# Summing the shift columns of w_ada two chunks at a time in a fused hybrid decoder layer

## The chip, the cores and the metric

The kernel runs on one core of one Trainium2 chip. The metric is the device time of one execution in microseconds (us). Before the change it is 1836.45 us, the median of three executions (1835.40, 1836.45 and 1836.54).

## The reference

One decoder layer over x of 1024 rows and 2048 columns, all in float32:

- `mod = silu(c) @ w_ada + b_ada`, cut into shift, scale and gate of 2048 numbers each; w_ada has 2048 rows and 6144 columns
- `h = rms_norm(x, norm_gain) * (1 + scale) + shift`
- `proj = h @ w_in` with 8192 columns: q, k, v, z of a stick-breaking attention (8 heads of 128) and of a chunkwise retention (8 heads of 128)
- both groups of heads, each multiplied by silu of its z
- `out = x + gate * (concat @ w_out)`

The change concerns the first line alone, and of it the 2048 numbers of shift.

## The kernel before

A float32 product is made of three matmuls on TensorE (PE): both operands are cut into a high and a low part, and high by high, high by low and low by high are added in one PSUM bank (`mm3`, L205 to L208). Cutting takes one copy on ScalarE (ACT, L193) and one subtraction on VectorE (DVE, L195).

Before the large projection the kernel computes seven heads' worth of columns (the retention's q, NZ = 7) directly, while it still prepares everything else. This is done in two passes of 16 steps each: the first over the upper 512 rows of x (L930), the second over the lower 512 rows (L1012). In step p of a pass, PE makes 7 times 3 matmuls with one 128-row piece of w_in (`start_mm`, the loop variable i counts the seven heads). Between them the second pass does the following, at fixed values of i:

- at the start of a step: load the two tiles of w_in of step p + 2 (`load_w`, tile name wr, called wr(p + 2) below), and in even steps a chunk of w_ada (`load_ada`). A chunk is 256 columns of w_ada in 8 tiles (name ada), each brought by its own DMA of 256 KB
- i = 0: four transposes of x into PSUM (`x_turn`, L601, tile xtp), copied out by ACT (L607); the copy of step p is that of x piece p + 2, called xT(p + 2)
- i = 2: the two parts of the scaled x piece (`make_h`, L652 on ACT, L654 on DVE)
- i = 3, even steps: `ada_mod`, which turns a chunk's sums by two transposes (L634) and reduces them on DVE (L637, L645) to 256 numbers of shift; in steps 2, 6, 10, 14 also `factors`, which queues further work that needs four pieces of shift
- i = 4, odd steps: `ada_sums` of the next chunk (L617 to L624): 16 matmuls of silu(c) with the chunk into one bank, four groups of 32 partitions, then a DVE copy of 128 by 256
- i = 4 and 6: cut wr(p + 2) (`cut_w`, L193 and L195)
- at most values of i: `pieces()`, one ACT and one DVE instruction of the queued work. Its parts end in stores of factors to DRAM (`store`, L382 and L383): for each k a pair B22h, B22l, then T1h, T1l, then T2h, T2l, called B22(k), T1(k), T2(k)

`x_turn`, `ada_sums` and `ada_mod` all write into the one PSUM bank with tag "C" (one buffer): each waits until the bank's former content has been read. In the second pass every engine's instructions, and the DMA issues on SyncE's queue (SP), run in the order in which the code states them (L982: `manual_schedule()`).

Of the 16 chunks the first eight give scale, the last eight (numbers 8 to 15) shift. Chunk 8 is summed in step 14 of the first pass and turned in step 0 of the second; chunk 9 is summed in step 1 and turned in step 2; chunk 8 + n is summed in step 2n - 1 and turned in step 2n. Chunks 8 and 9 are loaded in the first pass, chunk 10 between the passes, chunks 11 to 15 at the start of steps 2, 4, 6, 8 and 10. SBUF tiles come from a list of 92 slots, the one free longest being taken first (`Slots`).

Of the kernel before, what the change touches and what calls it, by code (L numbers as in the profile page):

```python
# [12 lines left out]
F32 = mybir.dt.float32  # L13
# [3 lines left out]
ALU = mybir.AluOpType  # L17

P = 128
S = 1024  # L20
D = 2048
KC = D // P
# [5 lines left out]
HALF = 512  # L28
# [23 lines left out]
CHUNKS = (0, 4, 1, 5, 2, 6, 3, 7)  # L52

KCS1 = (0, 1, 2, 3, 8, 9, 10, 11, 4, 5, 6, 7, 12, 13, 14, 15)
CHUNKS1 = (0, 1, 4, 5, 2, 3, 6, 7)
# [7 lines left out]
class Slots:  # L63
# [21 lines left out]
    def get(self, name, cls=None, dtype=F32, borrow=False):  # L85
        assert self.free, (name, cls, self.used)
        if cls in ("raw", "ring") and self.share and not (borrow or self.loose):
            assert self.used.get(cls, 0) < self.share[cls], (name, cls, self.used)
        i = self.free.popleft()
        self.used[cls] = self.used.get(cls, 0) + 1  # L90
        t = self.pool.tile([P, HALF], dtype, tag=f"s{i}", name=name)
        self.of[id(t)] = (t, i, cls)
        return t

    def put(self, *tiles):
        for t in tiles:
            _, i, cls = self.of.pop(id(t))
            self.used[cls] -= 1
            self.free.append(i)
# [3 lines left out]
def layer_kernel(ctx, tc, x, c, w_ada, b_ada, norm_gain, w_in, sb_q_gain, sb_k_gain, ret_norm_gain, w_out,  # L103
                 rot, ret_mask, ret_kdec, chunk_decay, out):
    nc = tc.nc
# [7 lines left out]
    sm = ctx.enter_context(tc.tile_pool(name="sm", bufs=2))  # L113
    om_pool = ctx.enter_context(tc.tile_pool(name="om", bufs=2))
    ps = ctx.enter_context(tc.tile_pool(name="ps", bufs=1, space=PS))
    dr = ctx.enter_context(tc.tile_pool(name="dr", bufs=1, space=bass.MemoryType.DRAM))
    get, put = slots.get, slots.put
# [25 lines left out]
    ident = cons.tile([P, P], F32, name="ident")  # L143
# [24 lines left out]
    gain_c = cols[:, 0:16]  # L168
    shift_b = cols[:, 16:32]
# [365 lines left out]
    shift = cons.tile([P, KC], F32, name="shift")  # L535
    qb = cons.tile([P, 2, NH], F32, name="qb")
    nc.vector.memset(qb, 0.0)
    ada, xT = {}, {}
# [6 lines left out]
    def load_ada(cc, gs=range(8)):  # L545

        col = (D + CHUNKS1[cc] * 2 * P) if cc < 8 else CHUNKS[cc - 8] * 2 * P
        for g in gs:
            ada[cc, g] = ar = get(f"ada_{cc}_{g}")
            nc.sync.dma_start(ar.rearrange("p (j n) -> p j n", n=2 * P),  # L550
                              ada_rows[:, 2 * g:2 * g + 2, col:col + 2 * P])
# [58 lines left out]
    silu_z = silu_t.rearrange("p (j n) -> p j n", n=32)  # L610
# [3 lines left out]
    def ada_sums(cc):  # L614


        ap_ = ps.tile([P, 256], F32, tag="C", name=f"accp_{cc}")  # L617
        for j in range(16):
            g = j % 4
            nc.tensor.matmul(ap_[32 * g:32 * g + 32, :], silu_z[:, j, :],  # L620
                             ada[cc, j // 2][:, (j % 2) * 256:(j % 2) * 256 + 256], start=j < 4, stop=j >= 12)
        put(*[ada.pop((cc, g)) for g in range(8)])
        acc = get(f"acc_{cc}")
        nc.vector.tensor_copy(acc[:, 0:256], ap_)  # L624
        return acc

    mods = cons.tile([P, KC], F32, name="mods")
    scale_b1 = cons.tile([P, KC], F32, name="scale_b1")

    def ada_mod(cc, acc):  # L630

        turned = ps.tile([P, 2 * P], F32, tag="C", name=f"mod_{cc}")
        for s in range(2):
            nc.tensor.transpose(turned[:, s * P:(s + 1) * P], acc[:, s * P:(s + 1) * P], ident)  # L634
        put(acc)
        mod = sm.tile([P, 2], F32, tag="mod", name=f"mod_s_{cc}")
        nc.vector.tensor_reduce(mod, turned.rearrange("p (s g r) -> p s g r", s=2, r=32)[:, :, :, 0],  # L637
                                mybir.AxisListType.X, ALU.add)
        k0 = 2 * (CHUNKS1[cc] if cc < 8 else CHUNKS[cc - 8])
        k2 = slice(k0, k0 + 2)  # L640
        if cc < 8:
            nc.vector.tensor_tensor(mods[:, k2], mod, scale_b1[:, k2], op=ALU.add)
            nc.vector.tensor_tensor(mods[:, k2], mods[:, k2], gain_c[:, k2], op=ALU.mult)
        else:
            nc.vector.tensor_tensor(shift[:, k2], mod, shift_b[:, k2], op=ALU.add)  # L645

    def make_h(p, hf):

# [122 lines left out]
    def start_mm(p, hf, ws, heads):  # L771
        kc = (KCS if hf else KCS1)[p]
        for h in heads:
            if p == 0:
                tag, bufs = starter_tags[h]
                first[h] = ps.tile([P, HALF], F32, tag=tag, bufs=bufs, name=f"first_{h}_{hf}")
            hi, lo = ws[h // 4]
            sl = slice(h % 4 * P, (h % 4 + 1) * P)
            mm3(first[h], hi[:, sl], lo[:, sl], h_hi[kc, hf], h_lo[kc, hf], p == 0, p == KC - 1)
# [110 lines left out]
    sums = {}  # L890
# [39 lines left out]
    for p in range(KC):  # L930
        c = p // 2
        if p == WRITTEN:
            written.close()
        loads(p)
        w = ws.pop(p)
        for h in range(NZ):
            start_mm(p, 0, w, (h,))
            if p < WRITTEN:
                s = p + 1
                if s < 4 and h == 2:  # L940
                    first_acc = first_sums(s)
                if s < 4 and h == 3:
                    first_mod(s, first_acc)
                    ws[s] = [cut_w(s, 0, raw[s], 0)]
                    make_h(s, 0)
                if p in (3, 5) and h == 1:
                    sums[c + 1] = ada_sums(c + 1)
                if p in (3, 5) and h == 2:
                    ada_mod(c + 1, sums.pop(c + 1))
                if (p, h) in TURNS:  # L950
                    x_turn(TURNS[p, h], 0, "C", 1)
                if (p, h) in SQUARES:
                    squares(SQUARES[p, h][0], SQUARES[p, h][1:])
                if s >= 4 and h == 4:
                    make_h(s, 0)
                    ws[s] = [cut_w(s, 0, raw[s], 0)]
                if h == (4 if s < 4 else 5):
                    ws[s].append(cut_w(s, 0, raw[s], 1))
                    put(*raw.pop(s))
                continue  # L960
            if (p, h) in TURNS:
                x_turn(TURNS[p, h], 0, "C", 1)
            if p >= KC - 2 and h == 1:
                x_turn(p - KC + 2, 1, "C", 1)
                make_h(p - KC + 2, 1)
            if p % 2 == 0 and h == 3:
                sums[c + 1] = ada_sums(c + 1)
            if p % 2 and p < KC - 1 and h == 0:
                ada_mod(c + 1, sums.pop(c + 1))
            if p == 12 and h == 3:  # L970
                norm_wide = norm_columns()
            if p == 13 and h == 5:
                norm_row = norm_rows(norm_wide)
            if h == 4 and p < KC - 1:
                make_h(p + 1, 0)
        put(h_hi.pop((KCS1[p], 0)), h_lo.pop((KCS1[p], 0)))
# [35 lines left out]
    for p in range(KC):  # L1012
        cc = 8 + p // 2
        if 2 <= p < KC - 2:
            rawz[p + 2] = load_w(p + 2, 1)
        if p and p % 2 == 0 and cc + 2 < 16:
            load_ada(cc + 2)
        if p >= 12:
            for _ in range(3):
                if early:  # L1020
                    b, hh, q = early.popleft()
                    load_raw(0, q, b, hh)
        w, cuts = ws.pop(p), []
        heads = range(NZ) if p < KC - 1 else (3, 0, 1, 2, 4, 5, 6)
        for i, h in enumerate(heads):
            start_mm(p, 1, w, (h,))
            if p == 1 and i or p > 1 and i < 2:
                scale_some(1)
            if i == 0 and p + 2 < KC:
                x_turn(p + 2, 1, "C", 1)  # L1030
            if i == 2 and p + 2 < KC:
                make_h(p + 2, 1)
            if i == 3 and p % 2 == 0:
                ada_mod(cc, sums.pop(cc))
            if i == 4 and p % 2 and cc < 15:
                sums[cc + 1] = ada_sums(cc + 1)
            if i == 3 and p % 4 == 2:
                factors((KCS[p - 2], KCS[p - 1]))
            if i in (4, 6) and p + 2 < KC:
                cuts.append(cut_w(p + 2, 1, rawz[p + 2], i // 2 - 2))  # L1040
            if i not in (2, 4):
                pieces()
            if p == KC - 1:
                if i:
                    spill(heads[i - 1], 1)
                if i in (1, 3, 5):
                    prepare_entry(i // 2)
        put(h_hi.pop((KCS[p], 1)), h_lo.pop((KCS[p], 1)))
        if p + 2 < KC:
            ws[p + 2] = cuts  # L1050
            put(*rawz.pop(p + 2))
# [658 lines left out]
    C = {2: (0, 0), 5: (1, 1), 3: (0, 1), 4: (1, 0)}  # L1710
# [281 lines left out]
    for i, (prod, ms, k) in enumerate(steps):  # L1992
# [16 lines left out]
        for m in ms:  # L2009
            for t in range(4):  # L2010
                b = 4 * m + t
                if k == 0 and prod not in (6, 5, 3):
                    tag, bufs = ("pj", 4) if prod == 7 else tags[b]
                    out_banks[b] = ps.tile([P, HALF], F32, tag=tag, bufs=bufs, name=f"y_{prod}_{b}")
                tk = slice(t * P, (t + 1) * P)
                for d in range(2 if both else 1):
                    l, r = lcut[i + d], rcut[i + d, m]
# [78 lines left out]
```

## Time and profile before

| what | value |
|---|---|
| median of three executions | 1836.45 us |
| the profiled execution | 1835.84 us |
| its span, first to last instruction | 1834.1 us |
| granted TensorE clock, mean | 0.999 |
| DVE busy | 1388.3 us (76%) |
| ACT busy | 872.4 us (48%) |
| main DMA queue, share of 16 engines | 88.0% |

The span is what lies between the first and the last instruction; 1.74 us of the execution lie around it. In a row of the timeline the first number is the start in us from the span's beginning and the second the time from the first start to the last end of the instructions merged in it. Successive matmuls overlap, so what a matmul costs is read from the distance between starts, not from its own duration. SPq rows are DMA issues: their length is the time to issue, and the data land later.

### The profile page before, as it was taken

What the parts mean: (1) busy time and instruction counts of PE and PEld (TensorE: products, weight loads), DVE (VectorE), ACT (ScalarE), POOL (GpSimd) and SP (SyncE); (2) the same over time, 40 slices, a digit from 0 to 9 for tenths busy, and PEclk for the clock granted to TensorE, in tenths of its full rate; (3) what the DMA queues carried; (4) which work ended last, traced back from release to release, by engine and by line L of the source; (5) the groups of instructions that cost most, each with busy time, mean ns of one, the idle gap of its engine ahead of it and who ended that gap; (6) DMA issues with size and microseconds to landing.
All of it is one profiled execution on the core that took longest, in us unless ns stands there. A gap on an engine that the chain in (4) does not pass through costs nothing.

```text
span 1834.1 us, 28370 instructions
## 1 busy us (share of the span) xinstructions
PE 1822.9 (99%) x9268; PEld 1501.3 (82%) x9268; DVE 1388.3 (76%) x2653; ACT 872.4 (48%) x1659; POOL 84.0 (5%) x226
## 2 busy tenths in 40 slices
PE   8999999999999999999999999999999999999999
PEld 6777788888888888878888888888888888888887
DVE  3578875666878777877778686988798777687697
ACT  3647852234554455435543554445545565452231
POOL 0000000000100010000010101000000001000000
PEclk9999999999999999999999999999999999999999
DMA  9998999998799699978997899889998864994694
GB/s 293 355 362 266 325 353 365 376 356 304 223 317 309 241 301 307 318 268 292 306 332 258 304 294 306 305 281 308 343 332 275 307 207 150 369 343 165 216 307 159
DMA packets 441112, 541.00 MB, mean 295 GB/s; under 512 B 33658, under 2 KB 246020, under 8 KB 440964
## 3 DMA queue, kind: packets, MB, share of 16 engines
q1 hardware_dynamic: 440148, 538.78, 88.0%
q8 instruction: 73, 1.20, 0.3%
q14 instruction: 75, 0.61, 0.1%
q10 hardware_dynamic: 816, 0.40, 0.1%
HBM read 448.83 MB, written 90.22 MB: 294 GB/s over the span
## 4 chain that ended last, share of the span: by engine, by line
PE 51%; ACT 0%; DMA 0%; DVE 0%; issue 0%; DVEq 0%
PE pj L206 10%; PE pj L208 9%; PE pj L207 9%; PE y L208 5%; PE y L206 5%; PE y L207 5%; PE sp L1577 1%; PE op L1596 1%; PE op L1598 1%; PE up L1559 1%; PE tp_B L1366 0%; PE oT L206 0%; PE oT L208 0%; PE oT L207 0%; PE zp L206 0%; PE zp L208 0%
## 5 line engine op out<-in xcount | busy, mean ns | idle before, releaser
L195 DVE TENSOR_TENSOR wl<-A,wh 128x512 fp32r<-128x512 f32 x392 | 270.6, 691 | 188.1 <-ACT wh L193 177.8
L193 ACT ACTIVATE wh<-A 128x512 fp32r<-128x512 f32 x392 | 247.1, 631 | 337.7 <-PE pj L207 319.8
L417 ACT ACTIVATE c<-pj 128x512 f32<-128x512 f32 x112 | 66.5, 598 | 120.8 <-PE pj L208 118.0
L316 DVE TENSOR_TENSOR A<-A,A 128x512 f32<-128x512 f32 x160 | 108.8, 686 | 1.7
L1330 ACT ACTIVATE om<-zp,y 128x128 f32<-128x128 f32 (+2 forms) x96 | 55.6, 579 | 104.1 <-PE zp L208 64.0
L421 DVE TENSOR_TENSOR c<-pj,c 128x512 f32<-128x512 f32 x104 | 69.8, 687 | 38.8 <-PE pj L208 38.6
L206 PE MATMUL first<-h_hi,wh_first 128*128 128x512 f32 x224 | 94.6, 423 | 0.8 <-ACT h_hi L652 0.8
L1346 DVE TENSOR_TENSOR_SCAN om<-om 128x128 f32<-128x128 f32 (+2 forms) x96 | 93.7, 976 | 1.1
L206 PE MATMUL pj<-T1h,wh 128*128 128x512 f32 x232 | 94.2, 406 | 0.0
L206 PE MATMUL pj<-B22h,wh 128*128 128x512 f32 x232 | 92.7, 400 | 0.0
L206 PE MATMUL pj<-B21h,wh 128*128 128x512 f32 x232 | 92.6, 399 | 0.0
L206 PE MATMUL pj<-B11h,wh 128*128 128x512 f32 x232 | 91.3, 393 | 0.0
L208 PE MATMUL pj<-T1h,wl 128*128 128x512 f32 x232 | 90.8, 391 | 0.0
L208 PE MATMUL pj<-B22h,wl 128*128 128x512 f32 x232 | 90.6, 391 | 0.0
L208 PE MATMUL pj<-B21h,wl 128*128 128x512 f32 x232 | 90.6, 391 | 0.0
L207 PE MATMUL pj<-B21l,wh 128*128 128x512 f32 x232 | 90.4, 390 | 0.0
L207 PE MATMUL pj<-T1l,wh 128*128 128x512 f32 x232 | 90.4, 390 | 0.0
L208 PE MATMUL pj<-B11h,wl 128*128 128x512 f32 x232 | 90.4, 390 | 0.0
L207 PE MATMUL pj<-B22l,wh 128*128 128x512 f32 x232 | 90.3, 389 | 0.0
L207 PE MATMUL pj<-B11l,wh 128*128 128x512 f32 x232 | 90.3, 389 | 0.0
L206 PE MATMUL pj<-T3h,wh 128*128 128x512 f32 x224 | 89.8, 401 | 0.0
L206 PE MATMUL pj<-T4h,wh 128*128 128x512 f32 x224 | 89.5, 400 | 0.0
(427 smaller groups left out, 4967.7 us busy)
## 6 DMA issues: line engine op xcount, KB each, us to landing
A<-in_w_in_dram SPq DMA_DIRECT2D x228, 256.0 KB, 5.6
ada<-in_w_ada_dram SPq DMA_DIRECT2D x112, 256.0 KB, 5.6
wB<-in_w_out_dram SPq DMA_DIRECT2D x112, 256.0 KB, 5.7
gr<-in_w_ada_dram SPq DMA_DIRECT2D x64, 256.0 KB, 5.5
T2h<-fac_T SPq DMA_DIRECT2D x56, 256.0 KB, 5.3
T2l<-fac_T SPq DMA_DIRECT2D x56, 256.0 KB, 5.8
T1h<-fac_T SPq DMA_DIRECT2D x56, 256.0 KB, 5.1
T1l<-fac_T SPq DMA_DIRECT2D x56, 256.0 KB, 5.5
```

What stands on the lines that cost most here:

```text
L193: nc.scalar.activation(hi[:, 0:n], src[:, 0:n], AF.Copy)
L195: nc.vector.tensor_tensor(lo[:, 0:n], src[:, 0:n], hi[:, 0:n].bitcast(F32), op=ALU.subtract)
L206: nc.tensor.matmul(o, a_hi, b_hi, start=first, stop=False, skip_group_check=on)
L207: nc.tensor.matmul(o, a_hi, b_lo, start=False, stop=False, skip_group_check=on)
L208: nc.tensor.matmul(o, a_lo, b_hi, start=False, stop=last, skip_group_check=on)
L316: nc.vector.tensor_tensor(r[o], r[a], r[b], op=ALU.add if n == 1 else ALU.subtract)
L417: nc.scalar.activation(order(t), o, AF.Copy)
L421: nc.vector.tensor_tensor(t, o, t, op=ALU.add)
L1330: nc.scalar.activation(om[:, :n], zp[:, :n], AF.Sigmoid, scale=y[:, 16 + i:17 + i])
L1346: nc.vector.tensor_tensor_scan(rev, rev, rev, init, op0=ALU.mult, op1=ALU.bypass)
L1559: nc.tensor.matmul(up[:, j * P:(j + 1) * P], kd[:, j * P:(j + 1) * P], vb(4 * g + j), start=True, stop=True)
L1577: nc.tensor.matmul(sp[:, j, :], r["k", g][:, tk], r["q", g][:, tk], start=True, stop=True)
```

## The change

`ada_sums2` sums two chunks of shift into one bank of 512 columns and copies them out in one instruction; `ada_shift2` turns both by four transposes, reduces them in one instruction and adds the bias in two. The two are called once in four steps of the second pass: the sums in steps 1, 5, 9 and 13 at i = 4, for chunks 8 and 9, 10 and 11, 12 and 13, 14 and 15; the turning in steps 2, 6, 10 and 14 at i = 3. Chunk 8 is no longer summed in the first pass. The loads move: chunk 11 from step 2 to step 3, chunk 12 from step 4 to step 5 (behind its sums), chunk 13 from step 6 to step 7, chunk 14 from step 8 to step 9 (behind its sums), chunk 15 from step 10 to step 11. Chunk 10 stays.

```diff
+    def ada_sums2(cc):
+        ap_ = ps.tile([P, HALF], F32, tag="C", name=f"accp_{cc}")
+        for d in range(2):
+            for j in range(16):
+                g = j % 4
+                nc.tensor.matmul(ap_[32 * g:32 * g + 32, d * 256:(d + 1) * 256], silu_z[:, j, :],
+                                 ada[cc + d, j // 2][:, (j % 2) * 256:(j % 2) * 256 + 256], start=j < 4, stop=j >= 12)
+            put(*[ada.pop((cc + d, g)) for g in range(8)])
+        acc = get(f"acc_{cc}")
+        nc.vector.tensor_copy(acc, ap_)
+        return acc
+
+    def ada_shift2(cc, acc):
+        turned = ps.tile([P, HALF], F32, tag="C", name=f"mod_{cc}")
+        for s in range(4):
+            nc.tensor.transpose(turned[:, s * P:(s + 1) * P], acc[:, s * P:(s + 1) * P], ident)
+        put(acc)
+        mod = sm.tile([P, 4], F32, tag="mod4", name=f"mod_s_{cc}")
+        nc.vector.tensor_reduce(mod, turned.rearrange("p (s g r) -> p s g r", s=4, r=32)[:, :, :, 0],
+                                mybir.AxisListType.X, ALU.add)
+        for d in range(2):
+            k0 = 2 * CHUNKS[cc + d - 8]
+            k2 = slice(k0, k0 + 2)
+            nc.vector.tensor_tensor(shift[:, k2], mod[:, 2 * d:2 * d + 2], shift_b[:, k2], op=ALU.add)
...
     first pass
-            if p % 2 == 0 and h == 3:
+            if p % 2 == 0 and h == 3 and p < KC - 2:
                 sums[c + 1] = ada_sums(c + 1)
...
     second pass
-        if p and p % 2 == 0 and cc + 2 < 16:
+        if p % 4 == 3 and p < KC - 1:
             load_ada(cc + 2)
...
-            if i == 3 and p % 2 == 0:
-                ada_mod(cc, sums.pop(cc))
-            if i == 4 and p % 2 and cc < 15:
-                sums[cc + 1] = ada_sums(cc + 1)
+            if i == 3 and p % 4 == 2:
+                ada_shift2(cc - 1, sums.pop(cc - 1))
+            if i == 4 and p % 4 == 1:
+                sums[cc] = ada_sums2(cc)
+                if p in (5, 9):
+                    load_ada(cc + 2)
             if i == 3 and p % 4 == 2:
                 factors((KCS[p - 2], KCS[p - 1]))
```

## Rows read from the trace of the kernel before

**Rows 1.** The page's part 1: busy us, share of the span, instructions.
```profile
PE 1822.9 (99%) x9268; PEld 1501.3 (82%) x9268; DVE 1388.3 (76%) x2653; ACT 872.4 (48%) x1659; POOL 84.0 (5%) x226
```

**Rows 2.** Windows of the second pass: stretch, busy us by engine, PEclk, DMA share, GB/s.
```profile
144.00:152.00 8.00, 8.00 (x63) 6.00 (x63) 7.13 (x12) 5.42 (x11) 0.00 (x0) 1.00 0.10 37
168.00:208.00 40.00, 40.00 (x260) 30.18 (x258) 30.77 (x57) 31.09 (x55) 0.00 (x0) 1.00 1.02 330
```

**Rows 3.** Timeline of PE around one chunk's sums: start, us, instruction, count.
```profile
130.80 0.39 PE L208 MATMUL first<-h_hi,wl_first 128*128 128x512 f32 x1
131.11 1.93 PE L620 MATMUL accp<-ada,silu_z 128*32 128x256 f32 x32
132.98 0.50 PE L206 MATMUL first<-h_hi,wh_first 128*128 128x512 f32 x1
133.31 0.40 PE L207 MATMUL first<-h_lo,wh_first 128*128 128x512 f32 x1
```

**Rows 4.** Timeline of PE, first pass: such a set with 128 columns.
```profile
23.43 1.08 PE L836 MATMUL accp_first<-ada_first,silu_z 128*32 128x128 f32 x32
24.44 0.50 PE L206 MATMUL first<-h_hi,wh_first 128*128 128x512 f32 x1
```

**Rows 5.** Timeline of PE: two transposes of sums, four of x.
```profile
150.51 0.38 PE L634 MATMUL mod<-ident,acc 128*128 128x128 f32 x2
150.65 0.48 PE L206 MATMUL first<-h_hi,wh_first 128*128 128x512 f32 x1
...
153.51 0.60 PE L601 MATMUL xtp<-ident,x 128*128 128x128 f32 x4
153.86 0.48 PE L206 MATMUL first<-h_hi,wh_first 128*128 128x512 f32 x1
```

**Rows 6.** Timeline of PE: the sums in steps 9 and 13.
```profile
182.49 1.93 PE L620 MATMUL accp<-ada,silu_z 128*32 128x256 f32 x32
...
208.17 1.93 PE L620 MATMUL accp<-ada,silu_z 128*32 128x256 f32 x32
```

**Rows 7.** Timeline of SP, DMA issues of steps 7 to 10.
```profile
167.91 0.90 SPq L756 DMA_DIRECT2D wr<-in_w_in_dram  x2
168.90 1.54 SPq L382 DMA_DIRECT2D fac_T<-T2h  x1
170.53 0.38 SPq L383 DMA_DIRECT2D fac_T<-T2l  x1
171.01 0.89 SPq L756 DMA_DIRECT2D wr<-in_w_in_dram  x2
172.00 4.09 SPq L550 DMA_DIRECT2D ada<-in_w_ada_dram  x8
...
179.47 0.34 SPq L383 DMA_DIRECT2D fac_B<-B22l  x1
179.87 0.92 SPq L756 DMA_DIRECT2D wr<-in_w_in_dram  x2
...
182.40 0.83 SPq L383 DMA_DIRECT2D fac_T<-T2l  x1
...
184.81 5.38 SPq L550 DMA_DIRECT2D ada<-in_w_ada_dram  x8
```

**Rows 8.** Timeline of ACT: three cuts of wr, one copy of xT behind.
```profile
172.27 0.63 ACT L193 ACTIVATE wh_first<-wr 128x512 fp32r<-128x512 f32 x1 [1.97 <-DMA wr<-in_w_in_dram]
...
177.00 0.62 ACT L193 ACTIVATE wh_first<-wr 128x512 fp32r<-128x512 f32 x1
...
198.52 0.63 ACT L193 ACTIVATE wh_first<-wr 128x512 fp32r<-128x512 f32 x1 [2.73 <-DMA wr<-in_w_in_dram]
...
200.89 0.58 ACT L607 ACTIVATE xT<-xtp 128x512 f32<-128x512 f32 x1
```

**Rows 9.** Transfers of tile wr from 90 to 235 us, issue to landing.
```profile
DMA to landing us min/median/max: 3.5/5.3/7.2
```

**Rows 10.** A window at the kernel's start, columns as in Rows 2.
```profile
13.00:16.00 3.00, 3.00 (x9) 2.46 (x10) 0.45 (x2) 0.00 (x0) 0.00 (x0) 0.50 1.11 314
```

More of the change, by code (lines that the diff above doesn't have):

```diff
@@ L638, in ada_mod @@
                                 mybir.AxisListType.X, ALU.add)
-        k0 = 2 * (CHUNKS1[cc] if cc < 8 else CHUNKS[cc - 8])
+        k0 = 2 * CHUNKS1[cc]
         k2 = slice(k0, k0 + 2)
[L641 to L645, printed above, removed]
+        nc.vector.tensor_tensor(mods[:, k2], mod, scale_b1[:, k2], op=ALU.add)
+        nc.vector.tensor_tensor(mods[:, k2], mods[:, k2], gain_c[:, k2], op=ALU.mult)
     def make_h(p, hf):
```

## The prediction, made before the run

> **What bounds the kernel now.** I read the busy table first. PE is busy for 99% of the span [rows 1] at a granted clock of 0.999, so it sets the end, and a microsecond of PE time saved or lost in the second pass is one of the whole. Then I read the second pass by windows: PE is busy for all of each stretch there, and the DMA engines work in two regimes [rows 2]. From 144 to 152 us they are nearly idle (share 0.10, 37 GB/s), because SP stands in order behind the store of B22(0), whose tile is not ready; from 168 to 208 us they are full (share 1.02, 330 GB/s). Last I read the timelines of SP and ACT around the chunks, because the change moves loads, and an engine that takes its work in order passes a late load on to whatever stands behind it.
>
> **PE's own work.** From the last matmul ahead of a chunk's sums to the first behind it 2.18 us pass, 130.80 to 132.98, and the next starts 0.33 later [rows 3]; plain matmuls start 0.23 apart, so a set costs 2.18 + 0.33 - 2 x 0.23 = 2.05 us. From its first matmul to the one behind it 1.87 us pass; for 128 columns in place of 256 it is 1.01 [rows 3, 4]. The 128 columns between them cost 0.86, so streaming takes 1.72 and opening and closing a set the other 0.33. A double set then costs 2 x 1.72 + 0.33 = 3.77, against 4.10 for two: 0.33 saved, four times, 1.3 us. Bounds: nothing, if PE also closes between the two halves, and 2.4 us, if only the starts counted (each set's 1.87 would then shrink by 0.6). I take 1.3, because two sizes of the same instruction give it.
>
> The transposes stay 16 in number. Two hold PE for 0.14 us, four for 0.35 [rows 5]; each group adds about 0.08 behind it, so two pairs cost 0.44 and a four 0.43: no gain. DVE does four copies of 512 columns for eight of 256 and four reductions less; PE waits for DVE nowhere in this pass, so I count nothing. Its waits for PE grow from about 1.9 to 3.8 us at a time but halve in number; if that cover were gone, the double set's extra 1.7 us would be late on DVE once per four steps.
>
> Until a double set comes, PE runs ahead of the old schedule. By the start of the sums in step 9 five single sets and five pairs of transposes have gone (chunks 8 to 12), and two double sets and two fours have come: 5 x 2.05 + 5 x 0.22 - 2 x 3.77 - 2 x 0.43 = 2.95 us ahead. By step 13 it is seven, seven, three and three: 3.3 us. So the sums of step 9 are due at 182.49 - 2.95 = 179.5, those of step 13 at 208.17 - 3.3 = 204.9 [rows 6].
>
> **The moved loads.** This is where I expect the time to go. In the old order an even step's wr stands in front of that step's chunk on SP: wr(10) at 171.01, then the chunk at 172.00 [rows 7]. In the new one chunks 13 and 15 are issued in steps 7 and 11, and chunk 14 at the end of step 9, so each stands in front of the next even step's wr. Chunk 12 moves from the front of the idle stretch [rows 2] to behind it, so the queue has one chunk more to carry while it is full.
>
> A chunk's 8 issues take 4.09 to 5.38 us [rows 7]; I take the middle, 4.7. From issue, wr(9) reached its cut 4.4 later, 167.91 to 172.27 [rows 7, 8]; I take 4.4, as that is a cut that waited for its load. The bounds are 3.5 and 5.3, the shortest and the median landing [rows 9]. ACT cuts wr in order at i = 4 and 6; the copy of xT, which frees bank C, stands four instructions behind. It ended 200.89 + 0.58 - 198.52 = 2.95 after such a cut began [rows 8]. I follow one chain with these:
>
> - wr(9) issued by 168.8; chunk 13 until 173.5; T2(1) 0.8 (two issues at 0.38; its own took 2.0, the slow bound) until 174.3; wr(10) at its cut at 178.7 (177.00 before [rows 8]); bank C free of xT(11) at 181.7. The sums of step 9 are due at 179.5 and need bank C: PE stalls 2.2 us.
> - B22(2)'s low part is subtracted on DVE behind the same cut: its store came 179.47 - 177.00 = 2.5 after it [rows 7, 8], now 181.2; wr(11) 0.4 later; wr(11), T1(2), T2(2) take 183.23 - 179.87 = 3.4 [rows 7], until 185.0; chunk 14 until 189.7; wr(12) at its cut at 194.1.
> - The same again: store of B22(3) at 196.6, wr(13) from 197.0 to 197.9, chunk 15 until 202.6, the four stores of T1(3) and T2(3) 2.4 until 205.0, wr(14) at its cut at 209.4, bank C free of xT(15) at 212.4. The sums of step 13 are due at 204.9: 7.5 us of stall in all, the 2.2 of step 9 included.
>
> Nothing gives this back: PE is full behind the pass. The sum is 7.5 - 1.3 = +6.2 us. With every link at its quick end (4.1, 0.8, 3.5, stores at 0.38) bank C is free at 206.9, and the sum is 2.0 - 1.3 = +0.7; with every link at its slow end (5.4, 2.0, 5.3) it is free at 218.3, and the sum is about +12. The quick end needs a full queue to be as quick as an empty one, so I stay near the middle. The other deadlines hold: by the median landing chunk 13's last tile lands at 173.5 + 5.3 = 178.8 for 179.5, chunk 15's at 207.9 for 212.4; wr(10) and wr(14) are needed by PE itself only two steps behind the cut.
>
> On the profiled execution (1835.84) this gives 1842.0; the median shown lies 0.6 above it, so I forecast 1842.6.
>
> **The rivals.**
>
> 1. *No stall, only the saving.* Bank C decides, in step 13: if wr(14) is on ACT by 204.9 - 2.95 = 202.0, the copy of xT(15) is out in time. For it: SP stood still for factor tiles from 144 to 152 [rows 2] and does so, more briefly, in each later round, slack that the chunks can fill. Against it: chunk 15 now stands between wr(13) and wr(14), 4.1 us at the least. It gives 1836.45 - 1.3 = 1835.1, the side on which the change is not slower.
> 2. *A small stall.* The chain runs mostly at its quick ends, or only step 13 stalls: 0.7 to 3.7 above the old time, about 1838.5.
> 3. *The stalls also cost the clock.* After PE had stood idle between its first groups, the window from 13 to 16 us shows a granted clock of 0.50, the 1.2 GHz level, with PE busy throughout [rows 10]; 3 us at half pace lose 1.5. If both stalls do this, 3.0 come on top: 1845.6. Against it: single stalls of 2 to 5 us are not the thin activity of the start, and no row of the second pass shows one. The Trainium skill, "TensorE: Matmul & The Clock Gate", Part 1, has the halved clock as the state that an idle array falls back to and that sustained work lifts; the start of this trace agrees. By that rule this rival is the one to expect where a stall is long.
> 4. *The change does not move the loads as read.* If the slots that chunk 12 takes came free only much later, SP would stand there too; by the list's order they are freed in steps 3 and 4, so I give it little.
>
> **How the numbers follow.** Forecast 0.47, rival 3 0.13, rival 2 0.18, rival 1 0.18, faster by a cause that I don't see, or rival 4, 0.04. A measurement here tells about 0.2% (3.7 us) from no change. Slower by more: forecast and rival 3, 0.60. Within: rivals 1 and 2, 0.36. Faster by more would take almost three times the saving: 0.04. The range runs from 1835.0, which holds rival 1, to 1846.0, which holds rival 3 and leaves out the slow end of the chain; the forecast's own range is 1840.2 to 1846.
>
> **What would show it.** Right: PE idle ahead of the double sums in steps 9 and 13 with the copy of xT as releaser, ACT waiting for wr at the cuts of steps 8, 10 and 12, bank C's copies late by 2 and more us, and a double set of 3.7 to 3.8 us. The DMA engines should idle some 6 us longer around 145 us (a chunk's 8 x 256 KB at 330 GB/s [rows 2] take 6.4). Wrong: sums that start without idle time in step 13, or a chunk's own data as the releaser. A time under 1836 would mean that SP's slack swallowed the chunks, and one over 1846 that the clock fell or that the delay runs on into the next stage.

## The result and the profile after

The changed kernel takes 1850.67 us (median of five executions, 1849.09 to 1852.96); the kernel before took 1836.37 in the same session. The ratio is 1.0079, 95% interval [1.0067, 1.0091]: slower by 14.3 us, where 6.2 were forecast, and outside the range. The profiled execution has a span of 1848.4 us.

The busy table (part 1 of the page, against [rows 1]) hardly differs. PE is busy 3.2 us longer and still reads 99%, in a span that is 14.3 longer:

```profile
PE 1826.1 (99%) x9268; PEld 1503.6 (81%) x9268; DVE 1386.4 (75%) x2645; ACT 871.2 (47%) x1659; POOL 85.3 (5%) x226
```

What PE waited for over the whole span, the first line of the view (total us, times, longest): the largest wait is one that the kernel before did not have at all, and its place is the double sums.

```profile
PE accp L636 <- ACT xT L607: 11.0, 2, 6.4
```

PE's timeline around the last three double sets and at the start of the large projection (start, us, instruction, count, in brackets the idle time ahead and its releaser; against [rows 3, 6]):

```profile
153.23 3.66 PE L636 MATMUL accp<-ada,silu_z 128*32 128x256 f32 x64
156.82 0.50 PE L206 MATMUL first<-h_hi,wh_first 128*128 128x512 f32 x1
...
183.19 6.55 PE L636 MATMUL accp<-ada,silu_z 128*32 128x256 f32 x64 [4.62 <-ACT xT L607]
189.68 0.50 PE L206 MATMUL first<-h_hi,wh_first 128*128 128x512 f32 x1
...
217.78 6.33 PE L636 MATMUL accp<-ada,silu_z 128*32 128x256 f32 x64 [6.37 <-ACT xT L607]
224.04 0.50 PE L206 MATMUL first<-h_hi,wh_first 128*128 128x512 f32 x1
...
235.55 0.39 PE L206 MATMUL pj<-B21h,wh 128*128 128x512 f32 x1
```

The set of step 5 (153.23) takes 3.59 us to the next matmul, as worked out: 1.87 for one chunk and 1.72 for the second. Those of steps 9 and 13 start late, behind waits of 4.62 and 6.37 us, and then take 6.49 and 6.26 for the same work. The windows say why (columns as in [rows 2]): the granted clock is 0.50 behind the first wait, the 1.2 GHz level, and 0.55 and 0.60 through the second set.

```profile
180.00:184.00 4.00, 0.81 (x8) 0.40 (x12) 2.76 (x5) 3.42 (x7) 0.00 (x0) 0.78 0.33 124
184.00:188.00 4.00, 4.00 (x44) 1.89 (x40) 1.56 (x3) 3.20 (x5) 0.00 (x0) 0.50 0.96 325
...
212.00:216.00 4.00, 0.00 (x0) 0.00 (x0) 0.18 (x1) 0.84 (x2) 0.00 (x0) 1.00 1.03 347
216.00:220.00 4.00, 2.23 (x24) 1.08 (x28) 3.38 (x6) 4.00 (x9) 0.00 (x0) 0.55 1.13 327
220.00:224.00 4.00, 4.00 (x48) 1.73 (x40) 0.76 (x2) 1.31 (x3) 0.00 (x0) 0.60 1.07 363
```

The copy of xT is only the last link. ACT's timeline, against [rows 8], shows it 1.99 us behind a cut of wr that had itself waited for its load: wr(10), wr(12) and wr(14), the three weights of even steps.

```profile
180.57 0.63 ACT L193 ACTIVATE wh_first<-wr 128x512 fp32r<-128x512 f32 x1 [5.63 <-DMA wr<-in_w_in_dram]
...
182.56 0.57 ACT L607 ACTIVATE xT<-xtp 128x512 f32<-128x512 f32 x1
...
197.85 0.63 ACT L193 ACTIVATE wh_first<-wr 128x512 fp32r<-128x512 f32 x1 [3.11 <-DMA wr<-in_w_in_dram]
...
215.16 0.63 ACT L193 ACTIVATE wh_first<-wr 128x512 fp32r<-128x512 f32 x1 [5.58 <-DMA wr<-in_w_in_dram]
...
217.15 0.57 ACT L607 ACTIVATE xT<-xtp 128x512 f32<-128x512 f32 x1
```

SP's issues, against [rows 7], show what stands ahead of these three loads: each time a chunk, and for wr(10) and wr(14) two and four stores behind it (at the "..."). The row at 182.56 is the store of B22(2)'s low part, which waited for the cut of wr(10); behind it in the queue stand wr(11), chunk 14 and wr(12), so the delay is passed on.

```profile
168.77 4.31 SPq L550 DMA_DIRECT2D ada<-in_w_ada_dram  x8
...
174.94 1.51 SPq L780 DMA_DIRECT2D wr<-in_w_in_dram  x2
...
182.56 0.33 SPq L383 DMA_DIRECT2D fac_B<-B22l  x1
...
186.09 4.99 SPq L550 DMA_DIRECT2D ada<-in_w_ada_dram  x8
191.19 1.06 SPq L780 DMA_DIRECT2D wr<-in_w_in_dram  x2
...
202.32 4.25 SPq L550 DMA_DIRECT2D ada<-in_w_ada_dram  x8
...
209.79 1.37 SPq L780 DMA_DIRECT2D wr<-in_w_in_dram  x2
```

Where the 14.3 us came from: the projection starts at 235.55 in place of 221.29, 14.26 later, and from there to the end it is 1612.8 us in both. Of the 14.26, the later start of step 13's sums is 9.61 (217.78 against 208.17), the double set, mostly at half pace, in place of the old single one 4.39 (6.26 against the 1.87 of [rows 3]), and the four transposes in place of two most of the 0.26 that is left.

### The profile page after: what moved, and what is told of

It is laid out like the page before. It is cut to its first block, busy times and chain, and to the rows that moved or that the text cites. A ratio compares the mean times of both kernels' runs of the same rounds, so it can differ in the third digit from the quotient of the medians.

```text
span 1848.4 us, 28357 instructions
## 1 busy us (share of the span) xinstructions
PE 1826.1 (99%) x9268; PEld 1503.6 (81%) x9268; DVE 1386.4 (75%) x2645; ACT 871.2 (47%) x1659; POOL 85.3 (5%) x226
## 4 chain that ended last, share of the span: by engine, by line
PE 50%; DVE 1%; ACT 0%; issue 0%; DVEq 0%
PE pj L206 9%; PE pj L208 9%; PE pj L207 9%; PE y L208 5%; PE y L207 5%; PE y L206 5%; PE sp L1603 1%; PE op L1622 1%; PE op L1624 1%; PE up L1585 1%; PE tp_B L1392 0%; PE oT L208 0%; PE oT L207 0%; PE oT L206 0%; PE zp L206 0%; PE zp L208 0%
```

## The experiments

Two theories stood at first. **A**: PE's own work is less, as forecast, and all of the loss is the new places of the loads. **B**: the pairing itself costs, since a double set holds bank C twice as long. Within A the next question was what about the loads does it, and how much of the loss is the clock's. Times are medians; each kernel has the kernel before of its own session beside it. The pass is read from the profiles, from the transposes of x at 66.72 us (66.08 after the change; ahead of all that the change touches) to the projection's first matmul: 154.57 us before, 169.47 after. What lies ahead of the pass differs between executions, by 4.1 us in e5's profile, whose transposes of x start at 70.82, so the last column and the times need not agree there.

| kernel | us | before | ratio, 95% interval | pass against before |
|---|---|---|---|---|
| the change | 1850.67 | 1836.37 | 1.0079 [1.0067, 1.0091] | +14.9 |
| e1 pairs, old loads | 1834.02 | 1835.51 | 0.9991 [0.9982, 1.0000] | -1.6 |
| e10 the same again | 1834.25 | 1835.45 | 0.9994 [0.9985, 1.0003] | -1.7 |
| e2 single sums, new loads | 1850.75 | 1835.51 | 1.0077 [1.0063, 1.0091] | +16.0 |
| e3 cut behind the copy | 1845.15 | 1835.51 | 1.0047 [1.0032, 1.0063] | +11.3 |
| e4 filler, 20 and 28 | 1849.47 | 1835.51 | 1.0074 [1.0060, 1.0087] | +14.5 |
| e9 filler, 20 and 20 | 1848.91 | 1835.45 | 1.0072 [1.0059, 1.0086] | +12.6 |
| e5 chunks 13, 15 back | 1844.65 | 1835.19 | 1.0055 [1.0040, 1.0070] | +7.6 |
| e6 chunk 12 back | 1849.56 | 1835.19 | 1.0078 [1.0063, 1.0093] | +14.2 |
| e7 wr ahead of the chunk | 1837.11 | 1835.19 | 1.0013 [1.0003, 1.0022] | -0.6 |
| e8 before, chunk ahead of wr | 1845.59 | 1835.19 | 1.0056 [1.0041, 1.0071] | +9.1 |

**e1 and e10: the pairing alone.** The double sums and fours of transposes stay, the loads go back to where they stood.

```diff
-        if p % 4 == 3 and p < KC - 1:
+        if p and p % 2 == 0 and cc + 2 < 16:
             load_ada(cc + 2)
...
-                if p in (5, 9):
-                    load_ada(cc + 2)
```

> Double sums and double turning as in the changed kernel, but the loads of chunks 11 to 15 stay at the start of steps 2, 4, 6, 8 and 10, as before the change. Theory A (the moved loads: a chunk ahead of the next even step's wr on SP makes that wr late, ACT cuts in order, bank C stays full, PE stalls): no stall in steps 9 and 13, double sets of about 3.6 us at full clock, 1835.0 to 1835.8 us. Rival B (the pairing itself: both chunks and bank C at one point, wherever the loads stand): stalls of 4 us and more in steps 9 and 13 stay, 1845 to 1851 us.

Measured: 1834.02, ratio 0.9991, under the 1835.0 to 1835.8 that theory A had. In e10's timeline of PE no set waits and all run at full pace:

```profile
178.48 3.66 PE L636 MATMUL accp<-ada,silu_z 128*32 128x256 f32 x64
...
203.75 3.66 PE L636 MATMUL accp<-ada,silu_z 128*32 128x256 f32 x64
...
218.85 0.39 PE L206 MATMUL pj<-B21h,wh 128*128 128x512 f32 x1
```

Theory B is out: the pairing costs nothing. Whether it gains was asked once more.

> The double sums and fours of transposes with the loads at their old places, once more in five rounds, since the first interval ended at 1.0000. The pairing theory: 1.3 to 1.5 us under the kernel before, ratio 0.9992. Rival: the first difference was the scatter of the runs, ratio 1.000.

Measured: 1834.25, ratio 0.9994. The executions put the gain at 1.5 and 1.2 us, with both intervals ending at about 1; the two profiles put the pass 1.6 and 1.7 shorter, where 1.3 were forecast. By its medians this version is the fastest of all that ran, faster than the kernel before by an amount that the timed executions barely tell from nothing.

**e2: the loads alone.** The single sums and pairs of transposes of before, with the chunks at the new places.

```diff
-        if p and p % 2 == 0 and cc + 2 < 16:
+        if p % 4 == 3 and p < KC - 1:
             load_ada(cc + 2)
...
                 sums[cc + 1] = ada_sums(cc + 1)
+                if p in (5, 9):
+                    load_ada(cc + 2)
```

> The kernel before with single sums at their old places, but with the loads of chunks 11 to 15 where the change puts them (steps 3, 5 behind the sums, 7, 9 behind the sums, 11). Theory A: wr(10) and wr(14) reach their cuts at about 180 and 210; PE is not 3 us ahead here, so the sums of step 9 (due at 182.5) wait 0 to 1 us and those of step 13 (due at 208.2) 3 to 6 us for bank C, 1840 to 1845 us. Rival B: no wait for bank C, 1836 to 1837 us.

Measured: 1850.75, more than any theory had, and as slow as the whole change. The first line of PE's waits and two of the three slow sets of its timeline:

```profile
PE accp L620 <- ACT xT L607: 10.2, 4, 4.2
```

```profile
187.20 3.57 PE L620 MATMUL accp<-ada,silu_z 128*32 128x256 f32 x32 [4.20 <-ACT xT L607]
204.46 3.47 PE L620 MATMUL accp<-ada,silu_z 128*32 128x256 f32 x32 [2.73 <-ACT xT L607]
```

Single sets, too, wait for bank C and then run at little over half pace, 3.2 to 3.6 us for the 1.93 of [rows 6]. The moved loads do all of it.

**e3: bank C let go ahead of the cut.** ACT cuts wr(10) and wr(14) only in the next step, behind the copy of xT.

```diff
-            if i in (4, 6) and p + 2 < KC:
+            if i in (4, 6) and p + 2 < KC and p not in (8, 12):
                 cuts.append(cut_w(p + 2, 1, rawz[p + 2], i // 2 - 2))
+            if i in (5, 6) and p in (9, 13):
+                ws[p + 1].append(cut_w(p + 1, 1, rawz[p + 1], i - 5))
...
```

> The changed kernel with all its loads where they are; only the two cuts of wr(10) move from step 8 (i = 4 and 6) to step 9 (i = 5 and 6), and those of wr(14) from step 12 to step 13, so that the copy of xT out of bank C no longer stands behind them on ACT. Theory A: wr lands as late as in the changed kernel, but PE no longer stalls ahead of the double sums, 1835 to 1837 us. Rival B, or data of the chunks that land late: the stalls stay at 3 us or more, 1843 us or more.

Measured: 1845.15, a miss. The sums no longer wait, but PE's timeline has a new wait behind them, for the cut weights themselves:

```profile
209.58 3.66 PE L636 MATMUL accp<-ada,silu_z 128*32 128x256 f32 x64
219.78 0.79 PE L206 MATMUL first<-h_hi,wh_first 128*128 128x512 f32 x1 [4.96 <-ACT wh_first L193]
220.37 0.63 PE L207 MATMUL first<-h_lo,wh_first 128*128 128x512 f32 x1
220.80 0.63 PE L208 MATMUL first<-h_hi,wl_first 128*128 128x512 f32 x1
```

Behind this wait full matmuls, and not a set of sums, run at half pace: from 220.37 to 224.21 they start 0.43 us apart in place of 0.23, and the granted clock from 220 to 224 is 0.50. So not only the sums run slow behind a wait, and e3 still pays for the clock, an estimated 2 us from these rows (ten starts, 0.2 more each).

So bank C is only the first thing that a late wr reaches. The load itself is too late: taking the bank out of its way gives 4.7 of the 14.3 us, and 3.6 of the pass.

**e4 and e9: is the slow clock a loss of its own?** Matmuls by a block of zeros, which add nothing, stand ahead of the sums of steps 9 and 13, so that PE goes idle for less time.

```diff
...
+            if i == 4 and p in (9, 13):
+                for n in range(FILL[p]):
+                    nc.tensor.matmul(first[h], zero, h_hi[KCS[p], 1], start=False, stop=False)
             if i == 4 and p % 4 == 1:
```

> The changed kernel with 20 matmuls by a zero matrix (128x512, they add zero to an open bank) ahead of the double sums of step 9 and 28 ahead of those of step 13, so that PE works in the time in which it stood idle: about 4.6 and 6.4 us at 0.23 us each. Theory C (the stall halves the clock of the set behind it): the double sets take 3.6 us instead of 6.5 and 6.3, clock 1.00, and the kernel is 4 to 6 us faster than the changed one, 1844 to 1847 us. Rival D (the clock falls because a double set of 32 columns is thin work in itself): sets of 6 us stay, 1850 us or more.

Measured: 1849.47, a miss, though both sets ran in 3.66 us: 28 fillers held PE some 1.4 us past the end of the copy of xT, at which the bank came free. So with 20 and 20:

> The changed kernel with 20 matmuls by a block of zeros (they add nothing to the sums of h) ahead of the sums in steps 9 and 13; at 0.23 us each they fill 4.6 us, about the 4.62 us wait of step 9 and 4.6 of the 6.37 us of step 13, so that PE goes idle for under 2 us at the end instead of over 6. Clock theory: step 13's set runs in 3.66 us instead of 6.33, and bank C comes free no later than in the changed kernel (217.8); the projection behind the pass starts 2.7 us earlier than the changed kernel's 235.55, about 232.9, and the time is 1848. Rival (the order of the loads sets when the second pass goes on, whatever the set's length): the projection starts at 235.5 and the time stays at 1850.7. A set of over 6 us behind so short a wait would reject the clock theory as I have it.

Measured: 1848.91. PE's timeline of e9 and the windows of its second set:

```profile
184.81 3.66 PE L639 MATMUL accp<-ada,silu_z 128*32 128x256 f32 x64
...
212.61 4.81 PE L1064 MATMUL first<-h_hi,zero 128*128 128x512 f32 x20
219.23 3.66 PE L639 MATMUL accp<-ada,silu_z 128*32 128x256 f32 x64 [1.80 <-ACT xT L610]
```

```profile
216.00:220.00 4.00, 2.20 (x23) 1.33 (x25) 2.72 (x5) 3.39 (x7) 0.00 (x0) 1.00 1.08 330
220.00:224.00 4.00, 4.00 (x61) 2.47 (x54) 2.64 (x5) 2.87 (x5) 0.00 (x0) 1.00 1.11 342
```

The clock stays at 1.00 and the pass is 2.3 us shorter than with the change: the 2.67 that step 13's set saves, less 0.33 by which bank C came free later. Step 9's set saves 2.9 as well, and it brings nothing, because PE then waits 1.41 us for xT at 209.36 and again for bank C. The timed executions alone don't tell e9 from the change (1.0072 and 1.0079, intervals overlap); the 2.3 us rest on the profile.

**e6 and e5: which chunk?** First chunk 12 back to step 4, ahead of the full stretch, to ask whether the amount in the queue does it; then the odd chunks 13 and 15 back to steps 6 and 10.

```diff
-        if p % 4 == 3 and p < KC - 1:
+        if p % 4 == 3 and p < KC - 1 or p == 4:
             load_ada(cc + 2)
...
-                if p in (5, 9):
+                if p == 9:
                     load_ada(cc + 2)
```

> The changed kernel with chunk 12 alone loaded at the start of step 4, ahead of the stretch in which the DMA engines idle, as before the change; chunks 13, 14 and 15 stay in steps 7, 9 and 11. Theory A1 (order): wr(10) and wr(14) still stand behind chunks 13 and 15, so the stalls of steps 9 and 13 shrink by 1 to 2 us at most, 1844 to 1850 us. Theory A2 (amount): with the chunk out of the full stretch the stalls mostly go, 1838 us or less.

Measured: 1849.56, with waits of 3.77 and 7.02 us ahead of the two sets. One chunk less in the full stretch changes nothing that these times can tell, so that chunk's amount is not it; e8, below, leaves the amount as it was.

```diff
-        if p % 4 == 3 and p < KC - 1:
-            load_ada(cc + 2)
+        if p in (3, 6, 10):
+            load_ada(11 if p == 3 else cc + 2)
```

> The changed kernel with chunks 13 and 15 loaded at the start of steps 6 and 10, behind that step's wr, as before the change; chunks 12 and 14 stay behind the sums of steps 5 and 9. Theory A1 (order: a wr issued right behind a chunk is late): wr(10) has no chunk right ahead of it, so no stall in step 9; wr(12) still has chunk 14 ahead, and through the stores of B22(3) wr(14) is some 4 us late, so a stall of 2 to 4 us in step 13 and a slow set behind it: 1838 to 1843 us. Theory A2 (amount: one chunk too many in the full stretch, whatever the order): stalls in both steps stay, 1847 us or more.

Measured: 1844.65, above what was expected. No wait of PE in the pass is over 1.6 us and the sets run in 3.66, so the clock's loss is gone; but there are now eight small waits between 180 and 218 us, 7.0 us in all, for weights, transposes and sums. Chunks 12 and 14 still stand right ahead of wr(8) and wr(12), and chunk 14's issue ends at 195.94 and wr(12)'s begins at 196.04.

**e7 and e8: the order alone.** e7 is the change with wr(10), wr(12) and wr(14) issued right ahead of chunks 13, 14 and 15; the chunks stay late. e8 is the kernel before with the two load statements of a step exchanged, and nothing else.

```diff
-        if 2 <= p < KC - 2:
+        if 2 <= p < KC - 2 and p not in (8, 10, 12):
             rawz[p + 2] = load_w(p + 2, 1)
+        if p in (7, 11):
+            rawz[p + 3] = load_w(p + 3, 1)
         if p % 4 == 3 and p < KC - 1:
...
                 sums[cc] = ada_sums2(cc)
+                if p == 9:
+                    rawz[12] = load_w(12, 1)
                 if p in (5, 9):
```

> The changed kernel with all chunks where they are; only the loads of wr(10), wr(12) and wr(14) are issued a little earlier, right ahead of chunks 13, 14 and 15 (in steps 7, 9 and 11). Theory A1 (order): wr is at its cut in time, no wait for bank C; at most a wait of 1 us for the last tile of chunk 13 in step 9: 1834.5 to 1838 us. Theory A2 (amount): wr or the chunks are late all the same, stalls of 3 us and more, 1842 us or more.

Measured: 1837.11, +1.9 in place of +14.3. PE's sums don't wait:

```profile
178.80 3.66 PE L636 MATMUL accp<-ada,silu_z 128*32 128x256 f32 x64
...
204.07 3.66 PE L636 MATMUL accp<-ada,silu_z 128*32 128x256 f32 x64
...
220.41 0.47 PE L206 MATMUL pj<-B21h,wh 128*128 128x512 f32 x1 [1.09 <-ACT T4h L686]
```

The saving is there until the projection, which begins with a wait of 1.09 for T4h; two more, 1.1 together, for cuts of its weights follow at 268 and 272 us. That is 2.2 of the 3.1 to 3.4 us between e7 and e1 or e10 (1.9 against -1.2 and -1.5); the rest was not traced.

```diff
+        if p and p % 2 == 0 and cc + 2 < 16:
+            load_ada(cc + 2)
         if 2 <= p < KC - 2:
             rawz[p + 2] = load_w(p + 2, 1)
-        if p and p % 2 == 0 and cc + 2 < 16:
-            load_ada(cc + 2)
```

> The kernel before, with one swap: in the even steps the chunk is issued ahead of wr(p + 2) and not behind it; steps, sums and everything else as before. Theory A1 (order): wr(10) and wr(12) reach their cuts 4 to 5 us later, bank C comes free about 1 us too late for the sums of step 9 and 2 us too late for those of step 11, later waits follow: 1838 to 1844 us. Theory A2 (amount), since the same data pass in the same stretch: 1836 to 1837 us.

Measured: 1845.59, +10.4, above the 1844 that theory A1 had as its upper end. SP, ACT and PE of e8 (their timelines) against [rows 7, 8, 6]:

```profile
174.25 4.13 SPq L550 DMA_DIRECT2D ada<-in_w_ada_dram  x8
178.48 0.89 SPq L756 DMA_DIRECT2D wr<-in_w_in_dram  x2
```

```profile
184.58 0.63 ACT L193 ACTIVATE wh_first<-wr 128x512 fp32r<-128x512 f32 x1 [4.79 <-DMA wr<-in_w_in_dram]
...
186.56 0.57 ACT L607 ACTIVATE xT<-xtp 128x512 f32<-128x512 f32 x1
```

```profile
187.19 3.42 PE L620 MATMUL accp<-ada,silu_z 128*32 128x256 f32 x32 [3.07 <-ACT xT L607]
```

The same bytes, sums and steps, with wr(10) behind the chunk: issued at 178.48 in place of 171.01, on ACT at 184.58 in place of 177.00 (1.15 of each difference is this execution's later start of the pass), and PE stalls and a single set takes 3.42 us for 1.93. The order of chunk and wr on SP is the cause, shown from both sides: put right in the changed kernel it takes away 12.4 of the 14.3 us, put wrong in the old one it costs 10.4.

## Why the prediction was wrong, step by step

**PE's own work: right.** The step 4 x 0.33 = 1.3 us was measured as 1.6 and 1.7 in the pass and 1.2 and 1.5 in the times; the double set took 3.59, as it has to by the sum. The transposes gave no gain, as said. Sums that nothing holds up start at 178.48 and 203.75 in e10, or 179.2 and 204.5 when its earlier start of 0.71 is added, for the 179.5 and 204.9 at which they were due.

**Where the stall appears: right.** Steps 9 and 13, the copy of xT as releaser, ACT waiting at the cuts of wr(10), wr(12) and wr(14), and nothing given back behind the pass.

**How late: this step failed.** Bank C was put at 212.4 us for step 13. It came free at 217.78, which is 218.4 by the clock of the trace before, as this execution was 0.64 ahead at the transposes: 6.0 too late. The term that was mis-sized is the landing of a wr that stands behind a chunk: 4.4 was taken, from wr(9). From issue to cut it measured 5.63 (174.94 to 180.57), 6.66 and 5.37, together 4.5 more. Another 1.3 was there before the first of them: wr(10) was issued at 175.6 by the same clock, for 174.3, as T2(1)'s two stores and the gaps around them took 1.9 in place of 0.8 and the chunk ended 0.2 later. The other links were off by up to 0.6 each, either way, and all but cancel.

The 4.4 was the shortest of three cuts that waited for their loads in this stretch of the kernel before. The other two are wr(11), 4.53 from its issue at 179.87 [rows 7], and wr(13), 5.03 from its issue to the cut at 198.52 [rows 8]; the two lines that show it, from ACT's and SP's timelines of before:

```profile
184.40 0.63 ACT L193 ACTIVATE wh_first<-wr 128x512 fp32r<-128x512 f32 x1 [1.25 <-DMA wr<-in_w_in_dram]
```

```profile
193.49 0.88 SPq L756 DMA_DIRECT2D wr<-in_w_in_dram  x2
```

Put in order of the time between the end of a chunk's issue and the issue of wr, the landings shorten: 6.66 us behind 0.1 (wr(12) after), 5.63 behind 1.9 (wr(10) after), 5.37 behind 3.2 (wr(14) after), 5.03 behind 3.3 (wr(13) before), 4.53 behind 3.8 (wr(11) before), 4.36 behind 5.9 (wr(9) before), and 3.2 to 3.4 behind about 10 (wr(9), wr(11) and wr(13) after). So the forecast took, of the three before, the wr that was farthest behind a chunk and used it for three that were near one. Its slow bound was 5.3, the median, where [rows 9] reach to 7.2.

The forecast's own slow end has bank C free at 218.3; the range left it out, and that is where it came free. That the two agree is in part luck: the slow end has chunks of 5.4 us, and the three here took 4.3, 5.0 and 4.3, while all three landings went past its 5.3. The median landing over all wr from 90 to 235 us, 5.5 after for 5.3, hides this.

**The clock: rival 3 was what happened, and it had a chance of 0.13.** It came true in both stalls. Its price was 2 x 1.5; the trace has 2.9 and 2.7, since most of a double set ran at half pace, and not three microseconds alone. Of these only the one of step 13 counts, 2.3 to 2.7 by e9. That of step 9 goes into the wait of step 13, which is set by the loads. The forecast had put this term at nothing. The Trainium skill, "TensorE: Matmul & The Clock Gate", Part 1, which stood beside this rival, has an idle array fall back to the halved clock; the stalls of 4.62 and 6.37 us here agree, with 0.50 to 0.60 granted behind them.

6.2 forecast, 6.0 for the later bank and 2.7 for the clock make 14.9, the difference of the passes. Rival 1 (SP's slack swallows the chunks), rival 2 (a small stall) and rival 4 are out; chunk 12 was issued at 153.29, right behind wr(7) and its own step's sums, so it did not stand for slots. The kernel of rival 1 is nearly possible, though: e7 keeps the chunks late, puts wr ahead of them, and loses 1.9.

**The signs.** The releaser, the cuts and the set of 3.7 came as named. From 135 to 155 us the DMA engines' share is 0.34 for 0.57 before, 4.6 us of idle time more, for the 6 that were named. The sign over 1846, the clock or a delay that runs on, read rightly: it was the clock and the loads.

**What stays open.** Why a wr close behind a chunk takes longer from its issue to its cut was argued, not tried. Two megabytes at the 330 GB/s of [rows 2] take 6.4 us and are issued in 4.3 to 5.0, so an estimate from these leaves 1.4 to 2.1 us of the chunk in the queue. For wr(12), the only one of the three right behind its chunk, that is 1.4 on top of the 3.3 or so of a wr far from one, 4.7 in all, where 6.66 was measured: the estimate falls short. And the order by distance is no rule: in e8 wr(10) and wr(12) both follow a chunk within 0.1 us and take 6.10 and 5.26, and its wr(9), 9.9 behind one, takes 4.56.

## What to carry to other kernels

On a queue that is issued in order, find which load has the next deadline, and let the bulk stand behind it: a bulk load whose data is needed late must not be issued ahead of a small one that is needed in two steps. A load moved "to where there is time" should be costed by what it then stands in front of. Where a stall on TensorE is forecast, price the work right behind it at half clock too, as it ran here behind stalls of 2.3 to 7 us, and count only the last such loss if a later wait takes in the earlier ones.

## What the runs showed of the hardware

Idle time of PE in this pass and the pace of what followed it, row by row. Behind 1.03 us (e4), 1.22 and 0.69 (e5) and 1.80 (e9) a double set of sums ran at full pace, 3.66 us. Behind 2.29 and 3.07 (e8) and 2.73, 3.12 and 4.20 (e2) a single set took 3.2 to 3.6 us for 1.93. Behind 4.62 and 6.37 (the change) and 3.77 and 7.02 (e6) a double one took 5.9 to 6.6 for 3.66, and behind 4.96 (e3) full matmuls started 0.43 us apart for 0.23. Most of each set was slow, and not only its first matmuls: 6.26 us in place of 3.59 is, as an estimate at half pace, three quarters of step 13's work in the change.

The mean granted clock of the span, 0.996 for 0.999, hides this: it is a loss of 5.6 us in two places. And a busy share of PE of 99% stands both in the kernel with no stall and in the one with 11 us of them: PE's busy time counts the slow sets as work.
